# Moving the switch of the weight pool and the first casts of the sliding-window attention in a fused encoder layer

## The chip, the core and the metric

The kernel runs on one NeuronCore of a Trainium2 chip. The core has five engines, each with its own instruction stream that it works off in order: PE (TensorE, matrix products; its weight loads are listed apart as PEld), DVE (VectorE), ACT (ScalarE), POOL (GpSimd) and SP (SyncE, which here only issues DMA transfers). They meet through semaphores. The metric is the time of one execution on the device in microseconds.

## The reference: what is computed

One inference step of a one-layer streaming encoder on 1024 prompt frames and 64 sample frames, model width 1024, all in float32. The layer is cut to what matters here:

```
xn = rms_norm(x, g_attn)
rq, rk, rv, rg, sq, sk, sv, ga, gb = split(xn @ w_in)
A = rms_norm(retention(rope(rq), rope(rk), rv)) * silu(rg)        # 4 heads of 256, states carried by blocks
B = sliding_window_attention(sq, sk, sv, bias, sinks)             # 16 heads of 64, 2 key/value heads, 192 keys
x += (sigmoid(ga) * (A @ w_ret_out) + sigmoid(gb) * (B @ w_swa_out)) @ w_mix_out
x += cross_attention(rms_norm(x), memory keys and values)         # memory: rms_norm(mem) @ w_mk, @ w_mv
x += swiglu(rms_norm(x))
y = rms_norm(x, g_final)
```

Outputs are y for both sets of frames, the retention states, the last 128 keys and values of the window, and the memory's keys and values.

## The kernel before, in words

**Precision.** Products are done at float32 accuracy by halves: `split` (L122) makes of an operand a high part, an ACT cast to fp32r (L123), and a low part, a DVE subtraction (L124). Each product is then three matmuls (high by high, high by low, low by high): `mm3` (L147 to L151) or, in the large projections, `multiply` (L205, L206, L208).

**Projections.** The 1088 frames are two halves of 544. A pair of output blocks is made by one Strassen scheme (`strassen`, L247): seven products P1, P2, P6, P5, P7, P3, P4 in this order, 24 matmuls each. The weights of a pair come in two raw tiles of 512 KB (`load_raws`, L834), are cast and split to seven operands (`weight_ops`, L166) in buffers `wq` of the pool `weights` (five of them in the projections), with POOL making the sums (L183 to L189). P1 is copied out of PSUM by ACT into `u1` (L255), which the sums u2, u5, u3 (DVE, L252) build on; these tiles are in the pool `fa`. Products use three PSUM pairs in turn, so the fourth product needs what the first one left to be copied out. A result goes through a `stage` tile (L571, then a multiplication by the norm at L577 and, for gates, an activation at L580) to DRAM.

**Order of the projections** (`project_phase`, L546): retention's v, k, q by head, each head followed by a group of sample queries and by `retention(h)` (L702); then the window's keys and values, the third group of sample queries (`project(pair("w_sq", 3), queries(3))`), and twelve gate pairs: w_ga, w_rg, w_gb, with `memory_phase` (L482) interleaved. In the program head 3's retention stands ahead of the last two of these, but its instructions run in between them and the first gate pairs.

**Retention** (`retention`, L702, and `ret_out`, L810): four blocks of 256 frames and a sample block of 64 per head. A block turns keys and values on PE (`pk`), scales them (kt L730 and L731, vb L739 and L740), makes scores `pss`, masks them on DVE (sf, L751), splits the result (ss), makes the block's contribution to the state (`pkv`) and the output `po`. `ret_out` squares and copies po on ACT (L819, L820), takes a root, multiplies (L825), turns the result back on PE (`pb`, L829) and stores it. Its tiles have one buffer each.

**Window attention** (`mix_phase` L849, `swa` L885): for 17 chunks c and two halves hf, `scores` (PE L948, then bias, maxima and exps on DVE and ACT, L961 to L972, and the division, on POOL, L976), `turn` (PE L990, copy pT L993) and `weigh` (PE L1006). The scores run two halves ahead of `weigh`. In between, `fill` hands out pieces of `filler` (L1059): 48 matmuls of the last memory head's values (`w_mv`), then 8 x 3 products A @ w_ret_out, in pieces of half a product. The operands of these (`ret`, from the gated retention results d_gate0 in DRAM, in chunks CH of columns) and the w_ret_out weights are split here, in the same way.

**Order of instructions.** The framework schedules: it lists the instructions of each engine in an order of its own from program order, priorities and its own estimate of times, then adds semaphores. `issue_after` forces an order. A DMA issue on SP or ACT also waits for the transfer eight back.

Of the kernel before, what the change touches and what calls it, by code (L numbers as in the profile page):

```python
# [19 lines left out]
P = 128  # L20
# [9 lines left out]
H = 4  # L30
# [79 lines left out]
class Kernel:  # L110
# [222 lines left out]
    def run(self):  # L333
        nc, tc, io = self.nc, self.tc, self.io
        with ExitStack() as ctx:
# [146 lines left out]
    def memory_phase(self, mp):  # L482
# [8 lines left out]
        room = lambda: mp.tile([P, 1024], F32, tag="mw", bufs=3, name="mw")  # L491
# [54 lines left out]
    def project_phase(self):  # L546
        nc, tc, io = self.nc, self.tc, self.io
        with ExitStack() as ctx:
            self.fp = ctx.enter_context(tc.tile_pool(name="fa", bufs=1, reuse_waits="tile"))
# [84 lines left out]
            with ExitStack() as rctx:  # L634
# [4 lines left out]
                for h in range(H):  # L639
# [20 lines left out]
            project(self.load_ops((io["w_sk"], io["w_sv"])), lambda i, t, o: self.store(self.d_skv[i, :, half(t)], o))  # L660
            project(pair("w_sq", 3), queries(3))
            steps = [0, 0, 0, 0, 1, 2, 2, 3, 3, 3, 2, 0]
            for idx, w, act in ((1, "w_ga", AF.Sigmoid), (0, "w_rg", AF.Silu), (2, "w_gb", AF.Sigmoid)):
                for m in range(0, KT, 2):
                    store = nc.scalar.dma_start if idx else self.store
                    put = lambda i, t, o, idx=idx, m=m, store=store: store(self.d_gate[idx][m + i, :, half(t)], o)
                    other = None if idx else lambda i, m=m: self.d_ret[m + i]
                    with tc.issue_after(project(pair(w, m // 2), put, act, other)):
                        for i in range(steps.pop(0)):
# [3 lines left out]
                            else:  # L673
                                next(memory)

# [173 lines left out]
    def mix_phase(self):  # L849
        with ExitStack() as ctx:  # L850
            filler = []

            def fill():
# [31 lines left out]
    def swa(self, ctx, fill):  # L885
        nc, tc, io = self.nc, self.tc, self.io
        if True:
# [4 lines left out]
            flat = [t.rearrange("p a b -> p (a b)") for t in self.ring_tiles(0, KT, "swin", F32)]  # L892
            kT, vT = flat[0][:, :KC], flat[5][:, :KC]
            bias = flat[2][:, :NPAIR * NKEY].rearrange("p (a b) -> p a b", b=NKEY)
            sinks = self.sinks
            qTs = [t[:, :16 * 2 * 64].rearrange("p (i c e) -> p i c e", i=4, c=4) for t in (flat[1], flat[7])]
            vts = [flat[4][:, i * P:(i + 1) * P] for i in range(17)] + [flat[0][:, KC + i * P:KC + (i + 1) * P] for i in range(3)]
            self.lds = [t[:, i * 384:(i + 1) * 384] for t in (flat[3], flat[6]) for i in range(5)]
            with tc.high_priority():
                def tokens(dst, i, cache):  # L900
                    self.load(dst[:, :SEQ], self.d_skv[i, :, :SEQ])
                    self.load(dst[:, SEQ:SEQ + P], io[cache])
                    self.load(dst[:, SEQ + P:], self.d_skv[i, :, SEQ:])

                tokens(kT, 0, "ckT")
# [797 lines left out]
```

## Time and profile before

| | |
|---|---|
| median of 3 runs | 2243.72 us (2242.51 to 2244.74) |
| the profiled execution | 2244.47 us |
| span in its trace | 2242.7 us |
| mean granted PE clock | 0.988 |
| share of the span: PE, DVE, ACT, POOL | 97%, 71%, 39%, 31% |
| DMA queues used | SP's (279.26 MB), ACT's (8.91 MB), and the instruction fetch |

The span counts from the first to the last instruction. A row of the trace's time line has the start, the duration, the engine, the line, the operation, what it writes `<-` what it reads with the shapes, and in brackets the idle time of the engine before it with what ended it. Buffer numbers are left out of names. Engines ending in q (SPq) are issue times of DMAs.

### The profile page before, as it was taken

The page shows a single profiled execution, that of the slowest core. Times are in us where ns is not written, and L with a number is a line of the kernel's source. Part 1 is how long each engine was busy: PE and PEld are TensorE (multiplying, and loading weights), DVE is VectorE, ACT ScalarE, POOL GpSimd, SP SyncE. Part 2 cuts the span into 40 slices and gives each one's busy share as a digit, 9 for nine tenths or more (in the row PEclk, how much of TensorE's full clock was granted, in tenths as well). Part 3 has the DMA queues.
Part 4 walks back from the last instruction along what each step waited for, and adds up shares of the span by engine and source line. Part 5 has one row for each costly group of instructions (what it writes and reads, how often), then busy time and mean ns, then how long its engine had stood idle before and what let it go on. Part 6 is the DMA issues. An engine that isn't in the chain of part 4 may idle for free.

```text
span 2242.7 us, 41756 instructions
## 1 busy us (share of the span) xinstructions
PE 2168.9 (97%) x16434; PEld 2105.3 (94%) x16434; DVE 1596.0 (71%) x2655; ACT 885.4 (39%) x1897; POOL 692.1 (31%) x466
## 2 busy tenths in 40 slices
PE   8899999999999989999999999999999999999986
PEld 8899999999999977779999998999999999999986
DVE  7986878666687667776455556668777677778587
ACT  7333333435444355554133333333323222344243
POOL 1441533342253112220000000014556555434462
PEclk9999999999999999999999999999999999999998
DMA  5533445443445475326443111422333332475233
GB/s 193 163 108 114 118 124 136 133 126 114 167 151 181 150 229 163 114 69 211 132 152 101 64 46 59 138 89 88 121 129 102 102 120 90 147 267 184 85 98 108
DMA packets 182599, 290.86 MB, mean 130 GB/s; under 512 B 40290, under 2 KB 110850, under 8 KB 182402
## 3 DMA queue, kind: packets, MB, share of 16 engines
q1 hardware_dynamic: 177794, 279.26, 39.3%
q10 hardware_dynamic: 4608, 8.91, 1.1%
q8 instruction: 130, 2.13, 0.4%
q14 instruction: 67, 0.55, 0.1%
HBM read 196.95 MB, written 91.16 MB: 128 GB/s over the span
## 4 chain that ended last, share of the span: by engine, by line
PE 79%; DVE 11%; DMA 5%; issue 2%; ACT 2%; POOL 1%; SPq 0%; DVEq 0%; ACTq 0%; POOLq 0%
PE pq L208 15%; PE pq L206 15%; PE pq L205 15%; PE pd L149 8%; PE pd L151 8%; PE pd L150 8%; DVE wq L124 2%; PE pout L1006 1%; DMA hl<-d_op 1%; PE pp L990 1%; PE pss L948 1%; DVE T L124 1%; DVE B L124 1%; DVE xg L1294 1%; DMA qs<-d_qkv 1%
## 5 line engine op out<-in xcount | busy, mean ns | idle before, releaser
L124 DVE TENSOR_TENSOR wq<-raw,wq 128x512 fp32r<-128x512 f32 (+1 forms) x505 | 448.8, 893 | 125.2 <-ACT wq L123 122.0
L123 ACT CAST wq<-raw 128x512 fp32r<-128x512 f32 (+1 forms) x505 | 307.5, 614 | 568.0 <-PE pq L208 259.1
L205 PE MATMUL pq<-T,wq 128*128 128x272 f32 x1832 | 492.9, 289 | 6.8 <-DVE u L252 3.6
L206 PE MATMUL pq<-T,wq 128*128 128x272 f32 x1832 | 493.0, 289 | 0.0
L206 PE MATMUL pq<-B,wq 128*128 128x272 f32 x1592 | 428.9, 289 | 9.1 <-DVE B L124 9.1
L205 PE MATMUL pq<-B,wq 128*128 128x272 f32 x1592 | 427.1, 289 | 0.2 <-ACT B L123 0.2
L208 PE MATMUL pq<-T,wq 128*128 128x272 f32 x1832 | 384.5, 290 | 3.4 <-DVE wq L124 3.4
L183 POOL TENSOR_TENSOR raw<-raw 128x512 f32<-128x512 f32 (+1 forms) x59 | 80.1, 1357 | 897.2 <-DVE rs_r L291 485.7
L205 PEld LDWEIGHTS pq<-T,wq 128*128 128x128 f32 x1832 | 346.1, 189 | 7.9 <-DVE u L252 3.7
L206 PEld LDWEIGHTS pq<-T,wq 128*128 128x128 f32 x1832 | 345.9, 189 | 0.3 <-issue 0.3
L208 PE MATMUL pq<-B,wq 128*128 128x272 f32 x1592 | 333.9, 290 | 0.0
L206 PEld LDWEIGHTS pq<-B,wq 128*128 128x128 f32 x1592 | 300.4, 189 | 11.0 <-DVE B L124 10.7
L205 PEld LDWEIGHTS pq<-B,wq 128*128 128x128 f32 x1592 | 300.2, 189 | 0.9 <-issue 0.4
L208 PEld LDWEIGHTS pq<-T,wq 128*128 128x128 f32 x1832 | 291.2, 190 | 4.6 <-DVE wq L124 3.8
L208 PEld LDWEIGHTS pq<-B,wq 128*128 128x128 f32 x1592 | 252.9, 190 | 0.5 <-issue 0.3
L252 DVE TENSOR_TENSOR u<-pq,u 128x544 f32<-128x544 f32 x177 | 127.6, 721 | 109.7 <-PE pq L208 109.2
L186 POOL TENSOR_TENSOR raw<-raw 128x512 f32<-128x512 f32 (+1 forms) x59 | 85.5, 1449 | 127.3 <-DVE wq L124 124.7
L976 POOL TENSOR_TENSOR t<-t,den 128x768 f32<-128x768 f32 (+2 forms) x34 | 47.9, 1408 | 170.7 <-DVE den L974 44.4
L571 DVE TENSOR_TENSOR stage<-pq,u 128x544 f32<-128x544 f32 x112 | 80.4, 718 | 26.4 <-PE pq L208 25.4
L184 POOL TENSOR_TENSOR raw<-raw 128x512 f32<-128x512 f32 (+1 forms) x59 | 87.3, 1480 | 3.7
L1461 POOL TENSOR_TENSOR y<-u,y 128x544 f32<-128x544 f32 x38 | 62.6, 1656 | 72.6 <-DVE y L1459 50.5
L189 POOL TENSOR_TENSOR raw<-raw 128x512 f32<-128x512 f32 (+1 forms) x59 | 83.3, 1412 | 4.4
(373 smaller groups left out, 4677.0 us busy)
## 6 DMA issues: line engine op xcount, KB each, us to landing
hl<-d_op SPq DMA_DIRECT2D x85, 272.0 KB, 4.6
d_qkv<-stage SPq DMA_DIRECT2D x44, 272.0 KB, 2.3
d_op<-stage SPq DMA_DIRECT2D x44, 272.0 KB, 2.4
d_op<-ht SPq DMA_DIRECT2D x44, 272.0 KB, 3.3
raw<-w_gate SPq DMA_DIRECT2D x22, 512.0 KB, 3.5
raw<-w_up SPq DMA_DIRECT2D x22, 512.0 KB, 3.6
d_gate<-stage ACTq DMA_DIRECT2D x32, 272.0 KB, 2.7
raw<-w_down SPq DMA_DIRECT2D x16, 512.0 KB, 4.2
```

What stands on the lines that cost most here:

```text
L123: self.last_cast = self.nc.scalar.copy(hi, src).ins
L124: return self.nc.vector.tensor_tensor(out=lo, in0=src, in1=hi.bitcast(F32), op=ALU.subtract).ins
L149: mm(ps, wh, xh, start=start, stop=False)
L150: mm(ps, wh, xl, start=False, stop=False)
L151: self.last_mm = mm(ps, wl, xh, start=False, stop=stop).ins
L184: tt(out=a21, in0=a21, in1=a22, op=add)
L186: tt(out=a11, in0=a22, in1=a11, op=sub)
L189: tt(out=a12, in0=a12, in1=a11, op=sub)
L205: mm(ps[:, c, :HC], w[:, 0, ks], x[:, 0, cs], start=start, stop=False)
L206: mm(ps[:, c, :HC], w[:, 0, ks], x[:, 1, cs], start=False, stop=False)
L208: self.last_mm = mm(ps[:, c, :HC], w[:, 1, ks], x[:, 0, c * HC:(c + 1) * HC], start=False, stop=stop).ins
L252: add = lambda out, a, b: nc.vector.tensor_tensor(out=out, in0=a, in1=b, op=ALU.add)
```

## The change

The weight pool and the pool `fa` are closed and opened again behind the third group of sample queries, with six `wq` buffers in place of five; before, six came only with the window attention. The memory phase has two `mw` buffers in place of three, and also loads and splits the last head's `w_mv`. A new `begin_swa` at the end of the projections loads the window's first tiles and, by `first_loads`, the first w_ret_out unit and the first 384 columns of its operand, with their casts; `first_low` takes their low parts to a place behind the second scores' maxima, and `later_operands` splits the other columns in halves among the later pieces. The order of the products goes over the columns for the first two output blocks, then block by block. `fill` hands out no pieces after the first scores and six after the second. The last gate pair's four stores and the four stores of the last memory head's values are issued by POOL.

```diff
@@ -371,26 +371,28 @@
                 self.rings = [Ring(sctx.enter_context(tc.tile_pool(name=f"ring{i}", bufs=1, reuse_waits="tile", side="right")))
                               for i in range(2)]
                 self.mem = sctx.enter_context(ExitStack())
-                with self.weights(5):
-                    self.project_phase()
-                with self.weights(6):
-                    with self.plain_psum():
-                        self.mix_phase()
-                        self.mem.close()
-                        self.cross_phase()
-                    rp = sctx.enter_context(tc.tile_pool(name="rf", bufs=1, reuse_waits="tile", side="right"))
-                    self.rstd_f = rp.tile([P, T], F32, name="rstd_f")
-                    self.temp = sctx.enter_context(ExitStack())
-                    self.new_b12(self.temp, side="right")
-                    self.cross_out_phase()
-                    self.ffn_phase()
-
-    @contextmanager
+                self.left = sctx.enter_context(ExitStack())
+                self.weights(5)
+                self.project_phase()
+                with self.plain_psum(side="right"):
+                    self.mix_phase()
+                    self.mem.close()
+                    self.cross_phase()
+                rp = sctx.enter_context(tc.tile_pool(name="rf", bufs=1, reuse_waits="tile", side="right"))
+                self.rstd_f = rp.tile([P, T], F32, name="rstd_f")
+                self.temp = sctx.enter_context(ExitStack())
+                self.new_b12(self.temp, side="right")
+                self.cross_out_phase()
+                self.ffn_phase()
+
     def weights(self, bufs):
+
+        self.left.close()
         self.wbufs = bufs
-        with ExitStack() as ctx:
-            self.wp = ctx.enter_context(self.tc.tile_pool(name="weights", bufs=2, reuse_waits="tile"))
-            yield
+        self.wp = self.left.enter_context(self.tc.tile_pool(name="weights", bufs=2, reuse_waits="tile"))
...
+    def sums_pool(self, ctx):
+        self.fp = ctx.enter_context(self.tc.tile_pool(name="fa", bufs=1, reuse_waits="tile"))
...
-        room = lambda: mp.tile([P, 1024], F32, tag="mw", bufs=3, name="mw")
+        room = lambda: mp.tile([P, 1024], F32, tag="mw", bufs=2, name="mw")
...
-        for h in range(H - 1):
+        for h in range(H):
             us = [self.unit(io["w_mv"][h, i], 4, 256, room) for i in range(2)]
+            if h == H - 1:
+                self.first_units = us
+                yield
+                return
...
-            self.fp = ctx.enter_context(tc.tile_pool(name="fa", bufs=1, reuse_waits="tile"))
+            fctx = ctx.enter_context(ExitStack())
+            self.sums_pool(fctx)
...
+            project(self.load_ops((io["w_sk"], io["w_sv"])), lambda i, t, o: self.store(self.d_skv[i, :, half(t)], o))
+            project(pair("w_sq", 3), queries(3))
+            fctx.close()
+            self.weights(6)
+            self.sums_pool(ctx)
...
-            project(self.load_ops((io["w_sk"], io["w_sv"])), lambda i, t, o: self.store(self.d_skv[i, :, half(t)], o))
-            project(pair("w_sq", 3), queries(3))
...
-                    store = nc.scalar.dma_start if idx else self.store
+                    store = nc.gpsimd.dma_start if (idx, m) == (2, KT - 2) else nc.scalar.dma_start if idx else self.store
...
+            next(memory)
+            self.begin_swa()
...
-                yield [pieces] * 4
                 yield []
-                count, steps, done = 48 - 8, 2 * 17, 0
+                yield [pieces] * 6
+                count, steps, done = 48 - 10, 2 * 17, 0
...
-                raws = [self.unit_raw(io["w_mv"][H - 1, i], 4, 256) for i in range(2)]
-                self.first_units = [self.unit_parts(raw, 4, 256) for raw in raws]
...
-                if hf == 0 and c % 4 == 0 and c + 4 < 17:
+                if hf == 0 and c % 4 == 0 and 0 < c < 13:
...
-                nc.vector.tensor_tensor(out=es, in0=snk, in1=nm, op=ALU.add)
+                ready = nc.vector.tensor_tensor(out=es, in0=snk, in1=nm, op=ALU.add).ins
...
-                nc.scalar.activation(es, es, AF.Exp)
+                self.marks.append((ready, nc.scalar.activation(es, es, AF.Exp).ins))
...
-                    with tc.high_priority(), tc.issue_after(self.operand_loaded):
-                        tokens(vT, 1, "cvT")
+                    with tc.high_priority(), tc.issue_after(self.last_operand):
+                        self.tokens(vT, 1, "cvT")
+                if i == 2:
+                    with tc.issue_after(self.last_operand):
...
+                        self.load_queries(qTs, 4)
                 if i == 8:
-                    with tc.issue_after(self.loaded):
+                    with tc.issue_after(self.last_operand):
...
+    def begin_swa(self):
+
+        tc, flat = self.tc, [t.rearrange("p a b -> p (a b)") for t in self.ring_tiles(0, KT, "swin", F32)]
+        self.flat, self.kT = flat, flat[0][:, :KC]
+        self.bias = flat[2][:, :NPAIR * NKEY].rearrange("p (a b) -> p a b", b=NKEY)
+        self.qTs = [t[:, :16 * 2 * 64].rearrange("p (i c e) -> p i c e", i=4, c=4) for t in (flat[1], flat[7])]
+        self.lds = [t[:, i * 384:(i + 1) * 384] for t in (flat[3], flat[6]) for i in range(5)]
+        with tc.high_priority():
+            self.tokens(self.kT, 0, "ckT")
+            self.load_queries(self.qTs, 0)
+            for e in range(2):
+                src = self.d_rb.rearrange("(p e) c -> e c p", e=2)[e, 63:63 + 64 * 255, :]
+                src = src.rearrange("(i c) p -> i p c", c=255)[:, :, :NKEY]
+                self.loaded = self.load(self.bias[e * 64:(e + 1) * 64], src)
+        self.rets = [self.rings[1].tile(f"ret{k}", slot=i) for k, i in enumerate((0, 1, 4, 5, 6, 7, 2, 3))]
+        self.marks = []
+        self.first_loads()
+
+    def tokens(self, dst, i, cache):
+        self.load(dst[:, :SEQ], self.d_skv[i, :, :SEQ])
+        self.load(dst[:, SEQ:SEQ + P], self.io[cache])
+        self.load(dst[:, SEQ + P:], self.d_skv[i, :, SEQ:])
+
+    def ld(self):
+        self.lds.append(self.lds.pop(0))
+        return self.lds[-1]
+
+    def first_loads(self):
+
+        nc, (c0, n) = self.nc, CH[0]
+        after, self.first = self.loaded, []
+        raw = self.unit_raw(self.io["w_ret_out"][0], KT)
+        for k in range(KT):
+            a = self.ld()[:, :n]
+            with self.tc.issue_after(after):
+                self.last_operand = self.load(a, self.d_gate[0][k, :, c0:c0 + n])
+            r = self.rets[k][:, :, c0:c0 + n]
+            self.first.append((a, r[:, 0], r[:, 1]))
+            nc.scalar.copy(r[:, 0], a)
+        qs = [self.new_op() for i in range(2)]
+        for i, q in enumerate(qs):
+            a = raw[:, i * 512:(i + 1) * 512]
+            nc.scalar.copy(q[:, 0], a)
+            self.first.insert(i * 5, (a, q[:, 0], q[:, 1]))
+        self.first_out = [(q[:, 0, i:i + P], q[:, 1, i:i + P]) for q in qs for i in range(0, 512, P)]
+
+    def first_low(self):
+
+        with self.tc.issue_after(self.marks[-1][0]):
+            for a, hi, lo in self.first:
+                self.nc.vector.tensor_tensor(out=lo, in0=a, in1=hi.bitcast(F32), op=ALU.subtract)
+
+    def later_operands(self, c0, n, ks):
+
+        a, b = self.marks[-1]
+        with self.tc.issue_after(a), self.tc.issue_after(b):
+            for k in ks:
+                x = self.ld()[:, :n]
+                with self.tc.issue_after(self.last_operand):
+                    self.last_operand = self.load(x, self.d_gate[0][k, :, c0:c0 + n])
+                self.split(x, self.rets[k][:, 0, c0:c0 + n], self.rets[k][:, 1, c0:c0 + n])
...
-            for c0, n in CH:
-                operands(c0, n)
+            ld, rets = self.ld, self.rets
+            self.first_low()
...
-                    nc.scalar.mul(o, ps[:, :256], self.mtok[:, t:t + 1])
-                self.store(self.d_mv[h, :, t, :], o)
-                self.store(io["o_mv"][t * P:(t + 1) * P, h * 256:(h + 1) * 256], o)
+                    self.values_out = nc.scalar.mul(o, ps[:, :256], self.mtok[:, t:t + 1]).ins
+                nc.gpsimd.dma_start(self.d_mv[h, :, t, :], o)
+                nc.gpsimd.dma_start(io["o_mv"][t * P:(t + 1) * P, h * 256:(h + 1) * 256], o)
...
-            for m in range(KT):
-                u = self.unit(io["w_ret_out"][m], KT)
-                for c0, n in CH:
-                    g = ld()
-                    self.load(g[:, :n], self.d_gate[1][m, :, c0:c0 + n])
-                    for ps in self.pieces(u, rets, c0, n):
-                        if ps is None:
-                            yield
-                    nc.vector.tensor_tensor(out=g[:, :n], in0=ps, in1=g[:, :n], op=ALU.mult)
-                    self.store(self.d_mix[m, :, c0:c0 + n], g[:, :n])
-                    yield
+            with tc.issue_after(self.values_out):
+                units = {0: self.first_out, 1: self.unit(io["w_ret_out"][1], KT)}
+            order = [(m, c) for c in range(3) for m in range(2)] + [(m, c) for m in range(2, KT) for c in range(3)]
+            halves = [range(4), range(4, KT)]
+            extra = {2: (1, 0), 3: (1, 1), 5: (2, 0), 7: (2, 1)}
+            step = 0
+            for m, c in order:
+                c0, n = CH[c]
+                if m not in units:
+                    units[m] = self.unit(io["w_ret_out"][m], KT)
+                u, g = units[m], ld()
+                self.load(g[:, :n], self.d_gate[1][m, :, c0:c0 + n])
+                for ps in self.pieces(u, rets, c0, n):
+                    if step in extra:
+                        i, j = extra.pop(step)
+                        self.later_operands(*CH[i], halves[j])
+                    step += 1
+                    if ps is None:
+                        yield
+                nc.vector.tensor_tensor(out=g[:, :n], in0=ps, in1=g[:, :n], op=ALU.mult)
+                self.store(self.d_mix[m, :, c0:c0 + n], g[:, :n])
+                yield
```

More of the change, by code (lines that the diff above doesn't have):

```diff
@@ L890, in swa @@
             mm = nc.tensor.matmul
[L892 to L896, printed above, removed]
[L897 to L913 removed]
+            flat, kT, bias, qTs, sinks = self.flat, self.kT, self.bias, self.qTs, self.sinks
+            vT = flat[5][:, :KC]
+            vts = [flat[4][:, i * P:(i + 1) * P] for i in range(17)] + [flat[0][:, KC + i * P:KC + (i + 1) * P] for i in range(3)]
             def keep():
@@ L1062, in filler @@
         if True:
-            def ld():
-                self.lds.append(self.lds.pop(0))
-                return self.lds[-1]
-            rets = self.ring_tiles(1, KT, "ret")
-            def operands(c0, n):
-                after = self.loaded
-                for k in range(KT):
-                    a = ld()
-                    with tc.issue_after(after):
-                        ins = self.load(a[:, :n], self.d_gate[0][k, :, c0:c0 + n])
-                    if c0 == 0:
-                        self.operand_loaded = ins
-                    self.split(a[:, :n], rets[k][:, 0, c0:c0 + n], rets[k][:, 1, c0:c0 + n])
-            for c0, n in CH:
-                operands(c0, n)
+            ld, rets = self.ld, self.rets
+            self.first_low()
             us, h = self.first_units, H - 1
```

6 lines of the change are left out of this document (removed).

## Prediction

> **What bounds the kernel now.** The head of the page comes first: does any engine fill the span?
>
> ```profile
> span 2242.7 us, 41756 instructions
> PE 2168.9 (97%) x16434; PEld 2105.3 (94%) x16434; DVE 1596.0 (71%) x2655; ACT 885.4 (39%) x1897; POOL 692.1 (31%) x466
> raw<-w_gate SPq DMA_DIRECT2D x22, 512.0 KB, 3.5
> ```
>
> PE is busy for 97% of the span, so only two things can move the time: the some 74 us in which PE has nothing to do, and the time it runs at a lower clock. The third line, from the page's list of DMAs, is the price of a 512 KB weight load, used below. Next, the busy time by windows (each row: length, then PE, PEld, DVE, ACT and POOL busy with their instructions, granted clock, DMA share, GB/s), at the two places that the diff touches: the pool switch after the third group of sample queries, and the start of the sliding-window attention (SWA).
>
> ```profile
> 510.00:540.00 30.00, 30.00 (x247) 30.00 (x246) 22.22 (x40) 19.37 (x36) 5.92 (x4) 1.00 0.36 114
> 540.00:580.00 40.00, 40.00 (x311) 38.10 (x311) 26.06 (x54) 20.28 (x37) 8.54 (x6) 1.00 0.42 128
> 800.00:815.00 15.00, 15.00 (x122) 15.00 (x122) 6.94 (x10) 2.44 (x4) 0.00 (x0) 1.00 0.82 245
> 820.00:840.00 20.00, 12.65 (x79) 11.61 (x80) 17.77 (x46) 16.68 (x53) 2.73 (x3) 0.76 0.91 309
> 840.00:855.00 15.00, 10.78 (x76) 8.11 (x74) 11.47 (x28) 9.43 (x32) 1.07 (x1) 0.95 0.96 298
> ```
>
> The first two rows are where head 3's retention runs interleaved with the first gate products: PE is full, at full clock. There is nothing to win there, and something to lose. The third row gives a price: 15.00 us for 122 product matmuls of 272 columns, 0.123 us each, 2.95 us for a product of 24. The last two are the head of SWA, where PE is busy 12.65 of 20 us and 10.78 of 15, while the DMA engines are nearly full (0.91, 0.96). PE's waits from 815 to 856 us say on what:
>
> ```profile
> PE pd L149 <- ACT wq L123: 8.2, 2, 6.3
> PE pp L990 <- POOL t L976: 2.2, 1, 2.2
> PE pout L1006 <- ACT pT L993: 2.1, 2, 1.1
> PE pss L948 <- DVE stage L571: 0.8, 1, 0.8
> PE pss L948 <- DVE t L961: 0.7, 1, 0.7
> PE pd L925 <- DMA swin<-d_skv: 0.3, 1, 0.3
> ```
>
> (Total, times, longest.) That is 14.3 us, 8.2 of it for casts of weights. The idle time costs more than itself. PE alone in windows of 3.4 us (length, busy, granted clock, DMA share, GB/s):
>
> ```profile
> 815.70:819.10 3.40, 0.89 (x10) 1.00 0.45 146
> 819.10:822.50 3.40, 3.06 (x12) 0.53 0.97 312
> ...
> 832.70:836.10 3.40, 0.00 (x0) 0.54 1.00 350
> 836.10:839.50 3.40, 2.92 (x9) 0.50 0.67 212
> ...
> 842.90:846.40 3.50, 2.50 (x19) 1.00 0.97 323
> ...
> 849.80:853.20 3.40, 1.50 (x12) 1.00 0.90 247
> 853.20:856.60 3.40, 2.38 (x9) 0.54 0.92 316
> 856.60:860.00 3.40, 3.40 (x13) 0.50 0.07 27
> ```
>
> After a window with 0.89, 0.00 or 1.50 us of work the next one runs at about half clock; after 2.50 us it doesn't, and once halved, 2.38 us do not bring it back. Four working windows ran at half: (3.06 + 2.92 + 2.38 + 3.40) / 2 = 5.9 us lost. **SWA's head costs 14.3 + 5.9 = 20 us.** That is all that this change can win there.
>
> **The change, part 1: SWA's head (a gain).** The 6.3 us wait is for the first output weights, whose cast comes late:
>
> ```profile
> 835.91 1.14 ACT L123 CAST wq<-raw 128x512 fp32r<-128x512 f32 x2 [0.97 <-DMA raw<-w_ret_out]
> ```
>
> ```profile
> 834.15 2.34 DVE L124 TENSOR_TENSOR ret<-swin,ret 128x384 fp32r<-128x384 f32 x3
> ```
>
> In the changed kernel these weights and the first 384 columns are loaded and cast during the last gate products, and the w_mv weights still earlier: both waits under `ACT wq` (8.2 us) go. What is late next? The ten low parts, on DVE behind the second scores' maxima: ten at 2.34 / 3 = 0.78 are 7.8 us. Beside them PE has the 48 value matmuls, 48 x 0.12 = 5.8 us, so 1 to 2 us shows. The POOL and pT waits (4.3 us) stay wholly, partly or not at all, since two scores now lie ahead; the 0.8 us stays. New: ACT casts the third weight unit ahead of the next exps, and its load goes out about 11 us after the last gate product; at 3.5 us, or twice that with the DMA engines full, PE may stand for 0 to 3 us there. Left: 0.8 + 1.5 + 2 + 1 = 5.3 us of idle and one half-clock window (1.7): 7, bounds 4 and 14. **Gain 20 - 7 = 13 us, bounds 6 and 16.**
>
> The last four d_gate2 stores and four d_mv/o_mv stores go to POOL's queue. The trace has no DMA from POOL. Bounds: nothing, as POOL's row from 800 to 815 shows 0.00 busy; or, if one holds POOL for as long as a 512 KB load takes, 4 x 3.5 = 14 us against the some 9 us that POOL has before its first multiply of SWA: 5 us. I take nothing, nearest to the empty row, and keep the 5.
>
> **Part 2: the switch (a loss).** The diff closes the weights and the pool `fa` and opens both anew, with six weight buffers, between the third sample group and w_ga. What that moves is seen in the order in which the changed kernel's instructions stand on each engine. Take t0 as the end of the third sample group's last product: some 508 us, one product (2.95) and its hops ahead of the copy at 511.30 below.
>
> ```profile
> 483.24 4.60 SPq L117 DMA_DIRECT2D raw<-w_ga  x2
> ...
> 505.28 4.28 SPq L120 DMA_DIRECT2D d_sq<-stage  x3
> ```
>
> ```profile
> 507.79 0.62 ACT L123 CAST qs<-qs 128x512 fp32r<-128x512 f32 x1 [1.83 <-DMA qs<-d_qkv]
> 511.30 0.60 ACT L255 COPY u<-pq 128x544 f32<-128x544 f32 x1
> 539.26 0.47 ACT L730 ACTIVATE kt<-pk,tok 128x256 fp32r<-128x256 f32 x1 [0.24 <-PE pk L699]
> 546.75 0.51 ACT L123 CAST ss<-sf 128x384 fp32r<-128x384 f32 x1 [1.66 <-DVE sf L751]
> 553.15 0.38 ACT L819 ACTIVATE ret_o<-po 128x256 f32<-128x256 f32 x1 [2.36 <-PE po L151]
> 558.34 0.91 ACT L825 ACTIVATE ret_o<-ret_o,rr 128x256 f32<-128x256 f32 x2 [1.71 <-DVE rr L298]
> 569.31 0.38 ACT L819 ACTIVATE ret_o<-pos 64x256 f32<-64x256 f32 x1 [1.25 <-PE pos L802]
> 570.20 1.28 ACT L290 ACT_TABLE_LOAD   x1
> ...
> 572.59 1.28 ACT L580 ACT_TABLE_LOAD   x1
> ...
> 574.80 0.49 ACT L825 ACTIVATE ret_o<-ret_o,rr 64x256 f32<-64x256 f32 x1
> ```
>
> ```profile
> 560.42 0.27 PE L699 MATMUL pk<-ident,small 128*64 128x128 f32 x1
> ```
>
> ```profile
> 514.25 0.48 DVE L731 SCALAR_TENSOR_TENSOR kt<-pk,tok,kt 128x256 fp32r<-128x256 f32 x1
> 520.61 0.74 DVE L751 SCALAR_TENSOR_TENSOR sf<-pss,rtok,dm 128x256 f32<-128x256 f32 x2 [0.34 <-PE pss L151]
> 523.13 0.55 DVE L124 TENSOR_TENSOR ss<-sf,ss 128x384 fp32r<-128x384 f32 x1
> ```
>
> Two moves matter. First, w_ga's raws were loaded 25 us ahead of t0 (483.24). Now SP issues the first one behind two d_sq stores that need the third group's third quarter, so at about t0 + 0.2; at 3.5 us, a cast and their hops the first product starts at t0 + 4.8, and PE has only some twelve transposes, 1.5 us, until then. Second, and dearer: the copy of the first product into u1 (before: at 511.30, between retention's steps) now stands on ACT behind all of retention's blocks 2 and 3 and the sample block of head 3, after the last multiply that was at 574.80. The fourth product (P5) reuses the PSUM pair that this copy empties (three pairs), so it waits for it; on PE everything between the third product and P5 is retention, a chain in which each step waits for the one before.
>
> How long is that chain at full clock? t0 + 4.8, then the 24 matmuls that stand ahead of block 2's scores, 3.7 with a wait for the low part: 8.5. Scores 12 x 0.12 = 1.4, sf 0.74, ss 0.51 and its low part 0.55, hops 0.6: 12.3. 26 matmuls to the end of po: 15.5. ret_o's multiply stands on ACT behind the next qs, whose load starts when po ends (3 us: a whole w_gate load takes 3.5), two casts 0.6 and the 0.91: 20.6. Transposes: 21.5. Block 3: kt and its low part twice (0.47, 0.48) and vb's alike, 3.8 less one overlap, 3.3; sf, ss and low part 1.8; po 21 x 0.12 = 2.5; hops 1.5: 9.1, so 30.6. Its ret_o (square, copy, root, small steps, 0.91): 3.5, so 34.1. The sample block: its ret_o lasts from 569.31 to 575.29, 6.0, less two table loads of 1.28 that fall away with the sigmoids between, 3.4; ahead of it 560.42 to 569.31, 8.9 between gate products, of which I take the steps themselves, 3.3 (estimate); 6.7 in all, and the copy's 0.60: 41.4. **P5 starts at t0 + 41.** PE's work in that time is three products (8.9), two blocks (2 x 6.6: 45 matmuls of 0.12 and twelve transposes) and the sample block (3.3, estimate): 25.4. So PE stands for 16 us, against none before.
>
> The upper end: in the trace block 3 took from 539.26 to 553.15, 13.9 us against my 9.1, and its ret_o from 553.15 to 559.25, 6.1 against 3.5, with gate products in between. If half of that excess, and of the sample block's 5.6, is the chain's own, it is 6 us more.
>
> Then the clock. From about t0 + 16 to t0 + 41 PE has 10 to 12 us of work in 25 us, 1.5 of each 3.4: the row of 849.80 (1.50, then 0.54). At half clock those 10 us become longer by up to 10, of which the steps on the chain are most: I take 6, bounds 0 and 12. P5 and what follows are full work as before, and nothing gives the time back, since PE was full in the rows up to 580 and again in that of 800 to 815. **Loss 16 + 6 = 22 to 23 us, bounds 14 and 34.**
>
> The Trainium skill, in "TensorE: Matmul & The Clock Gate", section "HAM oscillation — how this bites in real kernels", gives as the rule that PE should have no idle gap over about 3.4 us. The row of 849.80 speaks against it as a bound: there the longest gap was 2.2 us, and the clock halved all the same. By that rule the pauses in the chain, of 2 to 3.4 us each, would leave the clock whole, and the loss would be 16; by the rows it is 22.
>
> What else: six weight buffers bring nothing between the switch and 815, as PE has no gap there to fill (its three busy rows); mw with two buffers in place of three hides under the same full PE (cost if not: one load, 3.5 us).
>
> **Sum:** +22.5 - 13 = +9.5 us against the profiled execution's 2244.47, 2254.0; it lies 0.75 above the median 2243.72. **Forecast: 2254 us, slower.**
>
> **Rivals.**
> - *A, the hold-up is short (faster).* If P5 starts before about t0 + 34 (loads land sooner, small steps overlap), PE stands for under 9 us and the clock holds for the most part; loss 8, gain 13 to 16: 2238. For it: my hops are estimates. Against: block 3 took 13.9 us and nothing in its chain got shorter. It decides below a loss of some 9 us.
> - *B, the clock stays whole through the hold-up.* Loss 16 to 17, gain 13: 2248, no change that can be told. For it: the retention steps spread PE's work evenly, perhaps over the 2 us that a window seems to need (it holds after 2.50, falls after 1.50). Against: 10 us of work in 25. The rule that the Trainium skill states, as told above, would give this time.
> - *C, SWA's head doesn't do what it says.* The casts come early, but the DMA engines are as full as before, and the late cast of the third weights ahead of the exps takes the place of the 6.3 us wait: gain 5. 22.5 - 5 = +17.5: 2262. For it: DMA shares 0.91 and 0.96. Against: the first operands' loads now lie ahead of them.
>
> **Chances.** Forecast (2249 to 2259) 0.50, C and a hold-up of over 30 us (2259 to 2270) 0.18, B 0.17, A 0.15. Under 0.2%, 4.5 us, a measurement of this kernel can't tell from no change: faster 0.15, same 0.17, slower 0.68. The range goes from -5 (a loss of 11 with the full gain of 16, which leaves out A alone) to +24 (a loss of 30 with the smallest gain of 6; the ends 34 - 6 = 28 need both at once): 2239 to 2268.
>
> **What would show it.** Right: around 510 to 555 us PE waits for retention's own steps and at last for the u1 copy (L255), and the product after that copy starts some 41 to 48 us behind the end of the third sample group; granted clock near 0.5 to 0.7 in windows there; and at SWA's head one or no half-clock window and waits of 4 to 8 us. Wrong: PE full between 510 and 560; or waits at the head that stay above 12 us, named after w_ret_out's casts.

## The result and the profile after

The changed kernel takes 2259.74 us (median of 6 runs, 2257.39 to 2268.6) against 2243.45 before (6 runs): ratio 1.0079, 95% interval 1.006 to 1.0098, 16 us slower. Run once more beside other kernels it took 2262.57 against 2242.58, ratio 1.0092 (1.0069 to 1.0115). The forecast was 2254, range 2239 to 2268. The profiled execution, 2257.39 us, is the fastest of its six.

The page of the changed kernel: more span, and of the 12.9 us only 6.9 are PE's.

```profile
span 2255.6 us, 41756 instructions
PE 2175.8 (96%) x16434; PEld 2107.2 (93%) x16434; DVE 1600.8 (71%) x2655; ACT 877.7 (39%) x1891; POOL 695.2 (31%) x474
```

The windows at the switch, the same as those shown of before, and the one after (length, then busy time of PE, PEld, DVE, ACT and POOL, granted clock, DMA share, GB/s):

```profile
510.00:540.00 30.00, 23.93 (x158) 22.59 (x157) 19.16 (x36) 13.75 (x30) 8.05 (x6) 0.80 0.33 105
540.00:580.00 40.00, 34.80 (x225) 30.31 (x225) 19.63 (x43) 13.99 (x29) 3.35 (x3) 0.83 0.45 147
580.00:600.00 20.00, 20.00 (x163) 20.00 (x162) 11.82 (x17) 6.77 (x11) 5.59 (x5) 1.00 0.31 109
```

PE was full at full clock here before; now it stands for 6.1 and 5.2 us and runs at 0.80 and 0.83. PE's waits between 480 and 600 us:

```profile
PE pb L841 <- ACT ret_o L837: 11.5, 4, 3.8
PE pk L711 <- DVE ret_t L843: 1.9, 2, 1.0
PE pss L149 <- DVE kt L743: 0.3, 1, 0.3
```

All 13.7 us are named after retention's steps, which wait for one another. ACT's and then PE's time line at the end of the hold-up:

```profile
555.59 0.51 ACT L837 ACTIVATE ret_o<-ret_o,rr 64x256 f32<-64x256 f32 x1 [1.90 <-DVE rr L298]
556.00 0.59 ACT L255 COPY u<-pq 128x544 f32<-128x544 f32 x1
```

```profile
556.15 0.47 PE L841 MATMUL pb<-ident,ret_o 64*128 64x64 f32 x2 [1.63 <-ACT ret_o L837]
556.64 0.60 PE L205 MATMUL pq<-T,wq 128*128 128x272 f32 x1
```

The sample block's multiply, the copy into u1 behind it, and P5 as soon as the copy is done. PE's first wait in the hold-up ends at 508.35 after 2.71 us, so t0 is 505.6 and P5 starts at t0 + 51.

Positions show what it cost in all. The copy into u1 of the fourth w_ga pair, before and after:

```profile
590.94 0.61 ACT L255 COPY u<-pq 128x544 f32<-128x544 f32 x1
```

```profile
615.48 0.61 ACT L255 COPY u<-pq 128x544 f32<-128x544 f32 x1
```

24.5 us late, and the last such copy ahead of the window attention (798.62 before, 823.72 after) is 25.1 us late. At the next one, in the last phase (1531.07 and 1543.67), it is 12.6. So the profile has **a loss of 25.1 us at the switch, and 12.5 us won behind it.** The waits of the changed kernel's PE from 838 to 885 us, the head of the window attention:

```profile
PE pss L942 <- DVE t L955: 2.2, 2, 1.5
PE pp L984 <- POOL t L970: 1.9, 3, 1.1
PE pout L1000 <- ACT pT L987: 1.5, 1, 1.5
```

The 8.2 us for casts of weights are gone. PE alone in 48 us from the same point of the program, in the kernel before and in the changed one (length, busy, clock, DMA share, GB/s):

```profile
812.00:860.00 48.00, 33.60 (x209) 0.83 0.78 257
```

```profile
837.10:885.10 48.00, 42.34 (x290) 0.93 0.79 251
```

14.4 us idle became 5.7, and half clock (busy time by what is missing of the clock) 5.7 became 3.0; but 4.4 us of waits stand in the 200 us behind this window, 0.4 before. The head's net gain is 7 to 8 us of the 12.5. Of the rest, 2.7 are idle time in the 470 us behind it (8.4 before, 5.7 after), which no edit touched; some 2 us have no place. In the second profile of the changed kernel the copy at 1531.07 of before stands at 1551.13, 20.1 us late behind the same 25.1: there the gain is 5.

### The profile page after: what moved, and what is told of

It reads as the page before. It is cut to its first block, busy times and chain, and to the rows that moved or that the text cites. A ratio compares the mean times of both kernels' runs of the same rounds, so it can differ in the third digit from the quotient of the medians.

```text
span 2255.6 us, 41756 instructions
## 1 busy us (share of the span) xinstructions
PE 2175.8 (96%) x16434; PEld 2107.2 (93%) x16434; DVE 1600.8 (71%) x2655; ACT 877.7 (39%) x1891; POOL 695.2 (31%) x474
## 4 chain that ended last, share of the span: by engine, by line
PE 75%; DVE 13%; DMA 5%; ACT 3%; issue 3%; POOL 2%; SPq 0%; DVEq 0%; ACTq 0%; POOLq 0%
PE pq L208 14%; PE pq L205 14%; PE pq L206 14%; PE pd L149 7%; PE pd L151 7%; PE pd L150 7%; DVE wq L124 2%; PE pout L1000 1%; DMA hl<-d_op 1%; PE pp L984 1%; PE pss L942 1%; DVE stage L578 1%; DVE T L124 1%; DVE B L124 1%; DVE xg L1348 1%
```

## The experiments

The theory from the prediction: the loss is the hold-up at the switch, the gain is the head of the window attention. What had to be told apart: whether the switch or the head's edits cost the time, why u1 is late, what half clock costs, and which edit brings the gain.

**The early switch alone**: the kernel before with the pool lines of the change and none of its edits of the attention.

```diff
...
+            project(self.load_ops((io["w_sk"], io["w_sv"])), lambda i, t, o: self.store(self.d_skv[i, :, half(t)], o))
+            project(pair("w_sq", 3), queries(3))
+            fctx.close()
+            self.weights(6)
+            self.sums_pool(ctx)
...
```

> The kernel before with the early pool switch alone (pool weights with six buffers and a new fa behind the third sample group, two mw buffers); the window attention's head as before. If the hold-up at the switch is the loss and the head's changes the gain, only the loss is left: the profiles put the copies into u1 of the fourth gate pair at 590.94 before and 615.48 after, 24.5 us, so about 2244 + 24 = 2268 us, PE waits on ret_o as after, and the waits on wq casts (8.2 us) and half-clock windows at the head as before. If the loss came from the head's changes (POOL's DMAs, the late third weights), this one lies within 5 us of before.

2261.19 us against 2244.54, ratio 1.0069 (1.0055 to 1.0083). The copy of the fourth pair stands where it does after:

```profile
615.52 0.61 ACT L255 COPY u<-pq 128x544 f32<-128x544 f32 x1
```

The loss is the switch's. But the total is 7 us under the 2268 expected: 48 us from the head on, with nothing edited there but that no pool is opened, read

```profile
836.80:884.80 48.00, 39.45 (x266) 0.86 0.85 269
```

8.6 us idle and 5.5 of clock, against 14.4 and 5.7 before. The expected waits on wq casts are gone too, though these casts stand where they stood in the program. The first cast of w_ret_out (before: at 835.91, in a row that the prediction shows):

```profile
842.06 0.62 ACT L123 CAST wq<-raw 128x512 fp32r<-128x512 f32 x1 [4.30 <-DMA raw<-w_ret_out]
```

It stands 18.7 us behind the last copy into u1 ahead of the attention (823.39 here), for 37.3 before (798.62), and its load goes out 9.7 us behind that copy, for 31.3. So the loads and casts come early by themselves once the kernel opens no weights pool at the head. That the pool held them is read from these rows: the six buffers that this kernel already has there, and the other side that its PSUM pool takes, came with it and were not varied alone.

**The switch behind the w_ga pairs.**

```diff
-            fctx.close()
-            self.weights(6)
-            self.sums_pool(ctx)
...
                 for m in range(0, KT, 2):
+                    if (idx, m) == (0, 0):
+                        fctx.close()
+                        self.weights(6)
+                        self.sums_pool(ctx)
...
```

The memory phase's pools open there too, and no longer ahead of w_ga.

> The changed kernel with the switch moved from the place behind the third sample group to the place behind the w_ga pairs, when head 3's retention has ended. If the loss is the hold-up by retention, it goes and the head's gain stays: 2244 - 13 = 2231 us, up to 2236 if the first w_rg weights come late by 3 to 5 us at the new place; no waits on ret_o between 500 and 560. If reopening the pools costs as such, wherever it stands, 2250 to 2257 and a gap of 15 us or more near 610.

2242.53 us, ratio 0.9992 (0.9983 to 1.0001): no change. The fourth copy is 1.8 us late, as in all of this run up to there. PE's waits from 480 to 640:

```profile
PE pq L205 <- ACT wq L123: 3.3, 1, 3.3
PE pq L208 <- DVE wq L124: 0.5, 1, 0.5
```

Retention's waits are gone; the first w_rg weights come late instead, and the copies behind them are 8.3 to 9.9 us late, 7 more than ahead of them. So both expectations are half right: most of the loss was retention's, and a reopening costs some 7 us here too.

**The rope tables in a pool of their own.**

```diff
-                self.ra = rctx.enter_context(tc.tile_pool(name="ra", bufs=1, reuse_waits="tile"))
-                rope = self.ra.tile([P, 2, T], F32, name="rope")
+                rp = rctx.enter_context(tc.tile_pool(name="rope", bufs=1, reuse_waits="tile"))
+                rope = rp.tile([P, 2, T], F32, name="rope")
+                self.ra = rctx.enter_context(tc.tile_pool(name="ra", bufs=1, reuse_waits="tile"))
```

> The changed kernel, switch where it is, with one thing moved: the rope tables, 8.7 KB a partition, get a pool of their own ahead of retention's pool ra. The memory is laid out as before to the byte, but the new fa now lies over the rope pool, whose last reader is long done, and not over ra. If u1 is late because its new memory belongs to a pool that retention still holds, u1's copy comes right behind the first gate product, and of the loss only the late first w_ga weights stay, 3 to 9 us with their half-clock window: 2234 to 2240 us. If the switch delays the gate products for another reason (six buffers, new pools), 2255 or more as after.

2241.98 us, ratio 0.9988 (0.9978 to 0.9999), 18 to 21 us under the changed kernel. No tile's address moved, and the switch stands where it stood. The fourth copy, and PE's waits from 480 to 640:

```profile
598.93 0.61 ACT L255 COPY u<-pq 128x544 f32<-128x544 f32 x1
```

```profile
PE pb L842 <- ACT ret_o L838: 2.9, 2, 2.7
PE pk L712 <- DVE ret_t L844: 1.2, 1, 1.2
```

The copy of the first pair stands at 524.32, for 511.30 before and 556.00 in the changed kernel: it is back between retention's steps. The loss is 8.0 us for the 24.5, and 1.7 of it stood there ahead of the switch already. What is left comes with the late first w_ga weights: their load goes out at 508.56 (483.24 before). The first gate product starts at 513.85, right behind these waits; until then PE has only retention's steps to do. It is about as much as at the other place. The time is 2 us above the 2234 to 2240 expected.

**fa on the other side, so that the weights pool lies over retention's.**

```diff
-            self.sums_pool(fctx)
+            self.sums_pool(fctx, side="right")
...
             project(pair("w_sq", 3), queries(3))
-            fctx.close()
             self.weights(6)
-            self.sums_pool(ctx)
...
+                    if (idx, m) == (0, 0):
+                        fctx.close()
+                        self.sums_pool(ctx)
...
```

The memory phase's pools open behind w_ga here too.

> The changed kernel with fa on the other side of the memory until w_ga ends, so that at the switch only the weights pool grows, now itself over retention's memory. If a pool's new tiles wait for all of what lay under the pool, then all w_ga weights wait for the end of retention, not just u1: PE has two blocks and the sample block, 16.5 us of work, in a chain of some 38 to 45, then waits for a load of 4 to 5 us: idle 27 to 33 and 8 of half clock, less the 13 of the head: 2266 to 2272 us. If only tiles that overlap wait (the sixth buffer), u1 is free and it comes near 2235.

2273.2 us, ratio 1.0121 (1.0103 to 1.0139), just above the 2266 to 2272 expected. The fourth copy stands at 625.15, 34 us late, and PE waits

```profile
PE pb L842 <- ACT ret_o L838: 12.8, 4, 5.1
PE pq L205 <- ACT wq L123: 5.3, 1, 5.3
...
```

Now the first weights of w_ga wait for the end of retention: their load goes out at 552.34, behind the sample block's multiply at 550.53, where it went out at 506.17 in the changed kernel. Yet, by the sizes in the program, the tile that is loaded first has the address that it had before, far from retention's. These two runs settle why u1 was late: **the tiles of a newly opened pool were put behind all that the pools under it still had to do**, not behind the tiles under them. By the same sizes u1's new place lies over old u2 and u3; only the last 4 KB of the new fa (in u3 and u5) lie over retention's pool, and there over the rope tables, long read.

**One pool of six buffers from the start** (on the changed kernel, then on the kernel of the first experiment; the three lines of the switch go too).

```diff
+        u1, u2, u5 = tile_of("u1", "u1"), tile_of("u2", "u2"), tile_of("u5", "u5")
...
+        u3 = tile_of("u3", "u1")
...
-                self.weights(5)
+                self.weights(6)
...
-            sf = ra.tile([P, BLK + P], F32, tag="sf", bufs=1, name="sf")
+            sf = ra.tile([P, BLK + P], F32, tag="o", bufs=1, name="sf")
...
-        small = ra.tile([P, 5, SMP], F32, tag="sf", bufs=1, name="small")
+        small = ra.tile([P, 5, SMP], F32, tag="ss", bufs=1, name="small")
```

> The changed kernel without any switch: six weight buffers from the first projection on, in one pool. The 4 KB come from u3 sharing u1's tile and from retention's masked scores and sample tiles sharing those of ret_o and ss. If the loss is only the switch's, the copies into u1 stay within 3 us of before up to 798.62 and the head's gain (7 us between 812 and 1060 in the profile after) shows whole: 2234 to 2238 us. If the shared tiles cost as much as they free, 2240 to 2246.

2234.99 us against 2243.67, ratio 0.9957 (0.9944 to 0.997); from 480 us on the copies up to 798.62 stand 2.1 to 3.6 us ahead of before. The same with the old head:

> The same one pool of six buffers in the kernel before, with the window attention's head as it was (its own late casts, values behind the first scores). The run with the early switch alone lost only 13.7 us of idle and half clock at the head against 20.2 before, though nothing was changed there but that no pool is opened at it. If that is the head's gain, this kernel is as fast as the one with the casts ahead, 2236 to 2240 us, and the edits of the head are worth 0 to 2 us. If the edits are worth what was forecast (13), it is 5 to 10 us slower than that one.

**2230.91 us, ratio 0.9942 (0.993 to 0.9954): the fastest of all, and faster than before by 13 us.** Its program has the old head, but the casts are not late any more: the first w_ret_out load goes out at 808.74 and its cast stands at 817.95, for 829.90 and 835.91 before, with the last copy into u1 at 798.62 in both.

```profile
817.95 0.62 ACT L123 CAST wq<-raw 128x512 fp32r<-128x512 f32 x1 [4.71 <-DMA raw<-w_ret_out]
```

PE's waits in 812 to 884 are

```profile
PE pss L953 <- DVE t L966: 5.6, 1, 5.6
PE pd L149 <- DVE stage L576: 4.4, 1, 4.4
PE pp L995 <- POOL t L981: 0.9, 2, 0.6
```

10.9 us in four pieces, where the edited head on the same pool has 11.2 us in ten. The edits of the head are worth nothing here: 4 us less than nothing by the medians, and the two intervals touch. The profiles of all runs say the same. From the last copy into u1 ahead of the attention to the next one (798.62 to 1531.07 before, 732.5 us) the ten profiles with the edited head take 720.0 to 729.0 us, 725.1 in the mean; the two with the old head and no pool opened at it take 725.2 and 724.8.

**One edit alone: w_mv split in the memory phase**, on the one pool with the old head.

```diff
-        for h in range(H - 1):
+        for h in range(H):
...
+            if h == H - 1:
+                self.first_units = us
+                yield
+                return
...
```

The head no longer loads these weights, and its loads of the bias table no longer stand behind them.

> One pool of six buffers and the head as before, but with one of the change's edits: the last memory head's w_mv is loaded and split in the memory phase. The first wait of the kernel with one pool and the old head, 4.4 us ahead of the values, goes; if nothing takes its place, 2226 to 2229 us; if the wait ahead of the next scores (5.6 us) grows by as much, 2230 to 2232 as without the edit.

2235.27 us against 2242.58, ratio 0.9965 (0.9951 to 0.9978). The wait ahead of the values is still there, 4.9 us, now behind ACT's casts of `ret`, and the wait for POOL's division is 2.7 us, for 0.9. A miss: the wait was not for w_mv's load.

**The stores off POOL**, twice: on the one pool and with the rope tables apart.

```diff
-                    store = nc.gpsimd.dma_start if (idx, m) == (2, KT - 2) else nc.scalar.dma_start if idx else self.store
+                    store = nc.scalar.dma_start if idx else self.store
...
-                nc.gpsimd.dma_start(self.d_mv[h, :, t, :], o)
+                self.store(self.d_mv[h, :, t, :], o)
```

> One pool of six buffers with the changed head, but the last gate pair's stores issued by ACT and the memory values' stores by SP, none by POOL. POOL's first division of the attention, 128x256, took 4.20 us after, against 0.77 before. If POOL's DMAs slow it, it takes 0.8 here and the time falls by 0 to 4 us. If the ten low parts that DVE makes back to back beside it slow it, it stays at 4.2 and the time within 2 us of the other; SP's loads may come 1 to 3 us later.

2233.29 us, ratio 0.9951 (0.9938 to 0.9965): no difference. The division took 0.61 us, but it took 0.61 with the stores on POOL too, on this pool; so this pair told nothing about the 4.20.

> The kernel with the rope tables in a pool of their own, and the eight stores issued by ACT and SP in place of POOL. With them on POOL its first division (128x256) took 4.19 us, lying in time beside ten low parts that DVE made back to back. If POOL's DMAs slow the division, it takes under 1 us here. If DVE's low parts do, it takes over 3 us where it lies beside them, and under 1 us where it doesn't.

2241.97 us (one execution). The division, in the kernel with the stores on POOL and then in the one without:

```profile
833.84 4.19 POOL L971 TENSOR_TENSOR t<-t,den 128x256 f32<-128x256 f32 x1 [3.60 <-DVE den L969]
```

```profile
829.23 0.77 POOL L971 TENSOR_TENSOR t<-t,den 128x256 f32<-128x256 f32 x1 [27.67 <-DVE den L969]
```

Both lie beside DVE's ten low parts (832.45 to 837.5 and 827.85 to 833.3), so the low parts need not slow it. But the stores on POOL with the low parts beside them need not either. The changed kernel, in its first and then in its second profile:

```profile
849.21 4.20 POOL L970 TENSOR_TENSOR t<-t,den 128x256 f32<-128x256 f32 x1 [3.59 <-DVE den L968]
```

```profile
851.47 0.76 POOL L970 TENSOR_TENSOR t<-t,den 128x256 f32<-128x256 f32 x1 [3.59 <-DVE den L968]
```

In both, POOL's last store was issued some 4 us ahead, and the low parts run beside the division. Of the seven profiles with that order, four have 4.2 us and three 0.74 to 0.77. In the four, DVE's next three low parts took 1.47 us, in the three 1.88: it looks as if at times POOL and at times DVE gives way. What decides it is open, and one execution without the stores can't tell. The Trainium skill, in "DMA: Bandwidth & Descriptors", section "SWDGE vs HWDGE vs iDMA", says that GpSimd itself writes the descriptors of its DMAs into SBUF, and that DVE locks it out there while it works in a certain mode; no run here shows the descriptors or the mode. The time of the kernel doesn't show the 4.2: the execution with it took 2257.39 us, the one with 0.76 took 2266.21.

**The clock.** Filling matmuls in head 3's last blocks; their results are overwritten.

```diff
         pb = self.bank("pb")
+        if h == H - 1 and t0 >= 4:
+            for i in range(12):
+                nc.tensor.matmul(pb[:, i % 2, :P], self.ones, self.ones, start=True, stop=True)
```

> The changed kernel with twelve matmuls of ones by ones added to PE ahead of each turn of ret_o in head 3's last two blocks and its sample block, into the bank that the turn then overwrites: work for nothing while PE waits, some 2.6 us each. The waits stay; only the clock can change. If half clock is 8 to 11 us of the hold-up, the granted clock from 527 to 558 rises from 0.5 to 0.8 to 0.9 and more, and the time falls by 3 to 8 us, to 2252 to 2257. If the chain is bound by ACT, DVE and loads and the clock costs nothing, 2259 to 2262.

2259.22 us, ratio 1.0062 (1.0046 to 1.0078). By the expectation that is a clock that costs nothing; but the profiled execution took 2253 us, the other three 2258 to 2261. So it was run again beside the changed kernel.

> The changed kernel once more, unchanged, beside the next one on the same chip: 2257 to 2261 us, and the copy into u1 of the first gate pair about 45 us behind that of before. Its profile gives the second sight of the clock in the hold-up: 0.5 to 0.8 between 527 and 560.

> The changed kernel with the filling matmuls, again: its profile had no half clock from 516 on and stood 7 us earlier behind the hold-up than the changed kernel's, but its other three executions were at 2258 to 2261. If half clock costs 7 us, the median lies 5 to 8 us under that of the changed kernel beside it. If the one profile was a lucky one, they lie within 2 us, and the clock's share of the hold-up is small outside the profiled executions.

2262.57 and 2256.69 us, ratios 1.0092 (1.0069 to 1.0115) and 1.0063 (1.0045 to 1.0081): 5.9 us less. PE alone in the hold-up, of the changed kernel and of the one with the filling:

```profile
527.00:545.00 18.00, 11.57 (x66) 0.72 0.18 54
545.00:557.00 12.00, 7.74 (x31) 0.73 0.23 72
```

```profile
527.00:545.00 18.00, 15.26 (x118) 1.00 0.22 66
545.00:557.00 12.00, 11.85 (x86) 1.00 0.47 143
```

With the filling the clock is whole from 527 on, and the fourth copy stands 17.9 and 18.2 us late in its two profiles, against 24.5 in both of the changed kernel's. So half clock from 527 on costs 6.5 us by the positions in the profiles. The second pair of medians agrees, but its intervals overlap; the first median (2259.22 against 2259.74) shows 0.5 us, and that stays unexplained.

## Why the prediction was right, point by point

- **The place and the mechanism of the loss** held: u1's copy behind all of head 3's retention, P5 behind the copy. The order of instructions told it; no row of before could. What I did not say is why the copy stood there; the rope tables' pool and fa on the other side answer it.
- **P5 at t0 + 41** was t0 + 51. I summed the chain at full clock and added the clock apart, so this is no second error, but the 41 to 48 us that I gave as a sign were missed by 3. The first gate product started at 512.05, t0 + 6.4 for the t0 + 4.8 forecast. PE alone from t0 to P5, of the changed kernel:

```profile
505.60:527.00 21.40, 17.73 (x124) 0.84 0.55 163
527.00:545.00 18.00, 11.12 (x65) 0.81 0.17 53
545.00:557.00 12.00, 8.57 (x25) 0.53 0.20 65
```

  It was idle for 51.4 - 37.4 = 14.0 us, for the 16 forecast. Of the 37.4 us of work, 9.0 are the price of half clock (busy time by what is missing of the clock), so at full clock it is 28.4, for the 25.4 forecast.
- **The clock, 6 us**, was about 11 (25.1 - 14.0). Busy time by what is missing of the clock, in windows of 3.4 us from t0 to 566.8, gives 10.7: 8.0 from 527 on, where I had looked and where the filling won back 6.5, and 2.6 ahead of it, where PE has few weights to work on, at a clock of 0.84. That part I left out. The loss of 22.5 was 25.1, inside its bounds of 14 and 34 (the low end of my range went by a loss of 11, below that bound).
- **Rival B, a whole clock,** fell. One wait was 3.85 us, the others 3.3 or less, and the clock halved behind those of 2.71 and 3.30 too. So the rule of the Trainium skill ("TensorE: Matmul & The Clock Gate", "HAM oscillation — how this bites in real kernels") that PE should have no gap over about 3.4 us is not enough here; the rows fit a share of work in each window, as those of before did.
- **The gain, 13 us,** is the term that was mis-sized: 7 to 8 at the head in the first profile, 16 to 20 us of net loss by the medians, so 5 to 9, and 7.3 in the mean of the ten profiles with this head. I counted the waits that the edits remove and one or two that follow. Ten smaller ones followed in the first profile. Rival C's mechanism is one of them, in ACT's time line of the changed kernel:

```profile
857.06 1.14 ACT L123 CAST wq<-raw 128x512 fp32r<-128x512 f32 x2 [5.83 <-DMA raw<-w_ret_out]
858.11 0.26 ACT L921 COPY swin<-pd 128x128 f32<-128x128 f32 x1
858.26 0.58 ACT L987 COPY pT<-pp 64x512 f32<-64x512 f32 x1
```

  The third unit's cast stood 5.8 us for its load with the copy of pT behind it, and PE waited 1.54 us for pT at 858.89, not the 6.3 of before. C as a whole (gain 5, 2262) came nearer than the forecast: 2259.74 lies in the stretch that I gave 0.18 (2259 to 2270), not in the one that I gave 0.50. The clock, 5 us too small, and the gain, 4 to 8 too large, erred the same way; only the idle time, 2 too large, made up for a little of it. So the forecast was low by 6 to 9 us, inside a range of 29.
- **What brings the gain** I had half wrong. It is the earlier loads and casts, as I said, but not the edits that move them: with no weights pool opened at the head they come 18 to 19 us earlier with the old head too. The early switch alone had the gain nearly whole, and the one pool with the old head is no slower than with the new one. In my sum "the switch" was only a loss.
- POOL's stores at nothing: right by the time. The division's 4.2 us in the first profile I hadn't seen coming; it is not there in the second.

## What to carry to other kernels

A tile pool that is closed and reopened is an order put on the instructions: look which pools lay under its new memory, and when they end, not which tiles. Where 4 KB could be found for one pool of full size, no reopening was needed. That was worth 13 us here, and the edits at the place where the wait showed added nothing to it. When a wait is taken away in a stage where several engines and the DMA are near their limit, price the stage by what it still has to do, not by the waits that go.

## What the runs showed that I had not expected

A chain of small steps with PE at two thirds busy (11.57 of 18 us) ran at a clock of 0.72; the same chain with useless matmuls between its steps ran at 1.00 and was 6.5 us shorter. POOL's 128x256 division, behind POOL's own DMA issues (some 0.55 us of POOL each) and beside DVE's low parts, took 4.2 us in four profiles and 0.74 to 0.77 in three, and the same kernel had both. The same kernel's executions lie within some 12 us (2236.73 to 2248.86 before): a single profile's time ahead of another's by 5 us is not a result.
